# Two layers of a hybrid decoder on one core: TensorE's operands at other places modulo 512 bytes

## The chip, the core and the metric

The kernel runs on one core of a Trainium2 chip. Its time is the device time of one execution in microseconds. Five engines of the core matter here: TensorE (PE in the profile, its weight loads as PEld), VectorE (DVE), ScalarE (ACT), GpSimd (POOL) and SyncE (SP), whose queue issues most of the DMAs. SBUF is the on-chip memory from which TensorE reads both operands of a matmul: the stationary one, which a weight load brings into the array, and the moving one, which streams through it.

## The reference, cut to what matters

The reference is a decoder trunk of two layers on 256 tokens with 1,024 features, all in float32. In each layer

```
xn = rmsnorm(h);  z = xn @ w_in            # 8,200 columns in all
y_b = mixer_b(z_b)                         # RWKV-7, dilated attention, mLSTM, HGRN2
h = h + (sum_b sigmoid(gate_b) * (y_b @ P_b)) @ w_out
h = h + (silu(gt) * u) @ w_down            # u, gt: convolved halves of rmsnorm(h) @ w_up
```

and a last rmsnorm gives the output. Nearly all of the arithmetic is in the products with w_in, the four P_b, w_out, w_up and w_down.

## The kernel before, in words

The activations lie with features on the 128 partitions and tokens along the free axis: a tile of 8 blocks of 256 tokens holds 1,024 features. For the products each operand x is split in two float32r tiles, hi (x rounded) and lo (x - hi), and a product is three matmuls that add up in one PSUM tile: hi x hi, hi x lo, lo x hi. The helper `mm3` issues them (L351 to L353). Weights come in 312 groups of at most 1,024 columns: SyncE's queue loads a group to `raw` (L291), ScalarE makes `hi` from it (L301), VectorE makes `lo` (L302). The groups go round through three raw tiles and four pairs of hi and lo; a queue of four split groups stands ahead of TensorE.

In most products the weights are stationary (128 x 128) and the activations move (256 columns). In the token products (`tok_group`: hgt, att, mlt) and in the last layer's w_down it is the other way round: the activations are stationary, and 512 columns of weights move (392 in att).

These are the sets of activations that TensorE reads in those products, with the names in the profile:

- xh, xl: the inputs before their norm is applied (tags A and B of the persistent pool; made by `norm_block`, L407 and L408). They feed rw, part of hgq and hgf, and the first up groups of each layer.
- sh, sl: the normed inputs (tags C and D; `split_scaled`). They feed the gates, at, ml, the token products and most of up.
- yh, yl: the mixers' outputs, for the projections pp.
- mh, ml_: the merged branches, for w_out (wo).
- ahi, alo: the gated half of the feed-forward part, for w_down (dn).

A stage's matmuls follow one another without other work between them, except where a mixer's small matmuls are put in: the mixers are generators, and a step of one is run after every second call of `step()`. In the stages up, dn and wo nothing is put in apart from the norm's few matmuls (psrf, psbf) and, in the last layer, transposes of h (pht).

SBUF is laid out by pools that stand one behind the other in each partition: constants, weights (raw, hi, lo), the persistent pool (which begins with pr0 and then an empty tile, pad0), small pools, and in each layer a pool of parameters, and behind it the mixers' pools or those of the feed-forward part. A tile's address is the sum of the sizes ahead of it. Five empty tiles stand ahead of tiles that TensorE reads: pad0 (L244, ahead of hT, acc and the sets xh, xl), padC (L442, ahead of sh, sl), pady (L537, ahead of yh, yl), padm (L576, ahead of mh, ml_) and pada (L1410, ahead of ahi, alo). Blocks of the activations are 1,024 bytes long, so all blocks of a set have the same place modulo 512. The blocks of the weights' hi and lo lie at 256 modulo 512, but for att: its second block of 392 columns starts 1,568 bytes behind the first, at 288.

Of the kernel before, what the change touches and what calls it, by code (L numbers as in the profile page):

```python
# [9 lines left out]
F32 = mybir.dt.float32  # L10
# [211 lines left out]
def trunk(tc, x, wst, prm, rows, lora, fing, cfd, cid, out, dbg=None, depth=DEPTH):  # L222
# [7 lines left out]
    pp = pool("persist", bufs=1)  # L230
# [10 lines left out]
    ident_t = cp.tile([128, 128], F32, name="ident_t")  # L241
    pr0 = pp.tile([128, 8], F32, name="pr0")

    pp.tile([128, 416 // 4], F32, name="pad0")  # L244
    hT = pp.tile([128, KB, T], F32, name="hT")
    cft = cp.tile([128, cfd.shape[1] - 128], F32, name="cft")
    cit = cp.tile([128, cid.shape[1]], I32, name="cit")
# [30 lines left out]
    def pad(pl, name, nbytes):  # L278

        pl.tile([128, nbytes // 4], F32, name=name)  # L280
# [32 lines left out]
    def w_next():  # L313
        i = ws["use"]
        ws["use"] += 1
        w_ahead(i + 6)
        while ws["split"] < min(i + 4, NG):
            with tc.high_priority(offset=W_OFF):
                w_split(ws["split"])
            ws["split"] += 1  # L320
        return his.pop(i)
# [6 lines left out]
    def step():  # L328
        beat["t"] += 100
        if beat["t"] < BEAT:  # L330
            return
        beat["t"] -= BEAT
        for e in list(bg):
            e[2] += e[1]
            while e[2] >= 100 and e in bg:
                e[2] -= 100
                try:
                    next(e[0])
                except StopIteration:
                    bg.remove(e)  # L340
# [14 lines left out]
    def ct_block(ps_out, hi, lo, kn, cols, c0, ah, al, k0=0, first=True, last=True, quiet=False):  # L355
        for k in range(kn):
            a = k * cols + c0
            mm3(ps_out, hi[:, a:a + 128], lo[:, a:a + 128], ah[:, k0 + k, :], al[:, k0 + k, :],
                first and k == 0, last and k == kn - 1)
            if not quiet and k % 4 == 3:  # L360
                step()
# [77 lines left out]

    def split_scaled(m, tmp):  # L440
        if m == 0:
            pad(pp, "padC", 448)  # L442
            X["s"] = (pp.tile([128, KB, T], F32R, name="sh", tag="C"), pp.tile([128, KB, T], F32R, name="sl", tag="D"))
        h, lo = X["s"]
        ac.copy(h[:, m, :], tmp)
        gp.tensor_tensor(lo[:, m, :], tmp, h[:, m, :].bitcast(F32), op=OP.subtract)  # L446

    def scaled_block(m, gcol, R, tmp):

        if m % 2:  # L450
            ac.activation(tmp, hT[:, m, :], AF.Copy, scale=gcol)
            gp.tensor_tensor(tmp, tmp, R, op=OP.mult)
        else:
            ve.scalar_tensor_tensor(tmp, hT[:, m, :], gcol, R, op0=OP.mult, op1=OP.mult)
        split_scaled(m, tmp)
# [36 lines left out]
    for l in range(depth):  # L492
        with ExitStack() as lx:
# [12 lines left out]
            with ExitStack() as mxs:  # L506
                mp = lambda name, **k: mxs.enter_context(tc.tile_pool(name=f"{name}{l}", **k))
# [26 lines left out]
                    ve.tensor_scalar(c_ka, P("ka", 0, 2), -1.0, 1.0, op0=OP.mult, op1=OP.add)  # L534
                    ve.tensor_scalar(c_mu, P("mu", 0, 7), -1.0, 1.0, op0=OP.mult, op1=OP.add)

                pad(mp("pady", bufs=1), "pady", 160)  # L537
                yp = mp("yp", bufs=2)
                gtp = mp("gtp", bufs=5)
                zp = mp("zp", bufs=1)  # L540
# [14 lines left out]
                def project(b, kn, m2, quiet=False):  # L555
                    hi, lo = w_next()
                    ps = pmm.tile([128, 2, T], F32, name=f"pp{b}{m2}", tag="mm")
                    for n in range(2):
                        ct_block(ps[:, n, :], hi, lo, kn, 256, n * 128, *res[b], quiet=True)
                    if not quiet:  # L560
                        step()
                    g = gts.pop((b, m2))
                    if b == 3 and m2 == 0:
                        mg["t"] = pp.tile([128, 8, T], F32, name="merged", tag="A")
                    sl = slice(m2 * 2, m2 * 2 + 2)
                    mo = mg["t"][:, sl, :]
                    if b == 3:
                        ve.scalar_tensor_tensor(mo, g, 1.0, ps, op0=OP.add, op1=OP.mult)
                        return
                    ve.scalar_tensor_tensor(g, g, 1.0, ps, op0=OP.add, op1=OP.mult)  # L570
                    if b:
                        gp.tensor_tensor(mo, mo, g, op=OP.add)  # L572
                        return
                    if m2 == 0:
                        mop = mp("mop", bufs=1)
                        pad(mop, "padm", 128)  # L576
                        X["m"] = (mop.tile([128, KB, T], F32R, name="mh"), mop.tile([128, KB, T], F32R, name="ml_"))
                    mh, ml_ = X["m"]
                    ve.tensor_tensor(mo, mo, g, op=OP.add)
                    ac.activation(mh[:, sl, :], mo, AF.Copy, scale=0.5)  # L580
                    ve.scalar_tensor_tensor(ml_[:, sl, :], mo, 0.5, mh[:, sl, :].bitcast(F32), op0=OP.mult, op1=OP.subtract)
# [779 lines left out]
                for m2 in range(4):  # L1361
                    project(3, 2, m2)
                    gates(1, (m2,))
# [14 lines left out]
                for m2 in range(4):  # L1378
                    project(1, 1, m2)
                    gates(2, (m2,))  # L1380
                for e in LAST:
                    if e[0] == "g":
                        gates(0, (e[1],))
                    else:
                        if e == (2, 0):
                            drain(gm)
                            sph.close()
                        if e == (0, 0):
                            drain(grw)
                        project(e[0], 2, e[1])  # L1390
# [16 lines left out]
            with ExitStack() as fxs:  # L1407
                fp = lambda name, **k: fxs.enter_context(tc.tile_pool(name=f"{name}{l}", **k))
                ap_ = fp("act", bufs=1)
                pad(ap_, "pada", 448)  # L1410
                ahi = ap_.tile([128, NJ, T], F32R, name="ahi")
                alo = ap_.tile([128, NJ, T], F32R, name="alo")
                fq = fp("ffq", bufs=2)
# [4 lines left out]
                for j in range(NJ):  # L1418
# [12 lines left out]
                    if j < JU:  # L1431
                        ps = (ps0, ps1)[j] if j < 2 else ct_group(f"up{j}", quiet=True, pool_tag="mx", a=u)
                        z = fq.tile([128, 2, T], F32, name="zf", tag="zf")
                        for cs_, p_ in ps:
                            ve.tensor_tensor(z[:, cs_], p_, bc2(R, cs_.stop - cs_.start), op=OP.mult)
                        if j == 0:
                            for m in range(8):
                                gp.tensor_tensor(xsc[:, m, :], xsc[:, m, :], R, op=OP.mult)  # L1438
                        elif j < 3:
                            for m in range(j * 4 - 4, j * 4):  # L1440
                                split_scaled(m, xsc[:, m, :])
                    else:
                        z = ct_group(f"up{j}", quiet=True, pool_tag="mx")[0][1]
# [117 lines left out]
```

## Time and profile before

| | |
|---|---|
| median of 3 runs | 959.06 us (953.47, 961.19, 959.06) |
| the profiled execution | 950.05 us, of which the span of its instructions 948.3 us |
| mean granted clock of TensorE | 0.994 |
| busy: TensorE / VectorE / ScalarE / GpSimd | 98% / 77% / 60% / 24% |
| HBM | 166 GB/s over the span |

The profile is of one execution. Busy time counts overlapping instructions once; matmuls are pipelined, so TensorE may be busy all the time and still start its matmuls at a faster or slower rate.

### The profile page before, as it was taken

Reading aid. Unit: us, or ns where it says so; the run is one execution under the profiler, and the core shown is the slowest. Engines: PE = TensorE matmul, PEld = TensorE weight load, DVE = VectorE, ACT = ScalarE, POOL = GpSimd, SP = SyncE. Lnnn points to the kernel's source line nnn. Section 1 sums busy time; section 2 is a strip of 40 time slices with the busy share of each in tenths; the row PEclk is TensorE's granted clock in tenths of the full one; section 3 lists DMA queues with packets and bytes.
Section 4 is the critical chain, followed back from the end, with each engine's and each line's share of the span. In section 5 each row is a group of like instructions: output and inputs, shape, how many; then the busy total and the mean of one; then the engine's idle time right before and its main releaser. Section 6 shows DMA issues by size and latency. Waiting matters only on the chain.

```text
span 948.3 us, 21794 instructions
## 1 busy us (share of the span) xinstructions
PE 925.2 (98%) x8880; PEld 874.9 (92%) x8880; DVE 727.2 (77%) x1148; ACT 564.5 (60%) x956; POOL 225.7 (24%) x230
## 2 busy tenths in 40 slices
PE   8899999999999999999999999999999999999996
PEld 6889999999999999999998899999989999999885
DVE  6899556678688998876688975668768889988643
ACT  7773454665466677665479444555745657766532
POOL 3500131111207722120051003101112474111002
PEclk9999999999999999999999999999999999999999
DMA  7544344445466466655655434443546646756651
GB/s 278 178 133 139 113 155 144 135 153 170 135 191 205 144 207 219 199 183 194 207 176 178 134 109 141 147 155 124 169 132 196 200 138 214 232 183 197 188 193 63
DMA packets 48979, 160.08 MB, mean 169 GB/s; under 512 B 5872, under 2 KB 7408, under 8 KB 48752
## 3 DMA queue, kind: packets, MB, share of 16 engines
q1 hardware_dynamic: 46800, 155.03, 50.3%
q10 hardware_dynamic: 1728, 2.62, 0.9%
q8 instruction: 69, 1.13, 0.5%
q0 software_dynamic: 352, 1.06, 0.4%
q14 instruction: 30, 0.25, 0.1%
HBM read 156.06 MB, written 1.05 MB: 166 GB/s over the span
## 4 chain that ended last, share of the span: by engine, by line
PE 75%; DVE 8%; ACT 5%; POOL 4%; DMA 4%; issue 3%; POOLq 0%; ACTq 0%; SPq 0%; DVEq 0%
PE up L353 6%; PE up L351 6%; PE up L352 6%; PE gate L351 6%; PE gate L352 5%; PE gate L353 5%; PE dn L351 4%; PE dn L353 4%; PE dn L352 4%; DVE lo L302 3%; DMA raw<-in_wst_dram 3%; POOL sl L446 2%; ACT hi L301 2%; POOL xsc L1438 2%; PE at L351 1%
## 5 line engine op out<-in xcount | busy, mean ns | idle before, releaser
L302 DVE TENSOR_TENSOR lo<-raw,hi 128x1024 fp32r<-128x1024 f32 (+4 forms) x316 | 375.9, 1195 | 156.0 <-ACT hi L301 147.2
L301 ACT CAST hi<-raw 128x1024 fp32r<-128x1024 f32 (+4 forms) x316 | 307.8, 978 | 268.1 <-PE gate L352 56.9
L353 PE MATMUL up<-sh,lo 128*128 128x256 f32 x544 | 150.8, 277 | 0.7 <-DVE lo L302 0.7
L351 PE MATMUL up<-sh,hi 128*128 128x256 f32 x544 | 150.4, 277 | 0.0
L352 PE MATMUL up<-sl,hi 128*128 128x256 f32 x544 | 150.3, 276 | 0.0
L351 PE MATMUL gate<-sh,hi 128*128 128x256 f32 x512 | 146.0, 285 | 0.0
L352 PE MATMUL gate<-sl,hi 128*128 128x256 f32 x512 | 142.9, 279 | 0.0
L353 PE MATMUL gate<-sh,lo 128*128 128x256 f32 x512 | 142.9, 279 | 0.0
L353 PEld LDWEIGHTS up<-sh,lo 128*128 128x128 f32 x544 | 102.1, 188 | 1.5 <-DVE lo L302 1.5
L352 PEld LDWEIGHTS up<-sl,hi 128*128 128x128 f32 x544 | 102.2, 188 | 0.0
L351 PEld LDWEIGHTS up<-sh,hi 128*128 128x128 f32 x544 | 102.1, 188 | 0.0
L351 PEld LDWEIGHTS gate<-sh,hi 128*128 128x128 f32 x512 | 96.3, 188 | 2.9 <-ACT hi L301 0.2
L352 PEld LDWEIGHTS gate<-sl,hi 128*128 128x128 f32 x512 | 96.2, 188 | 0.9
L353 PEld LDWEIGHTS gate<-sh,lo 128*128 128x128 f32 x512 | 96.2, 188 | 0.6
L1463 POOL TENSOR_TENSOR af<-sf,cvf 128x256 f32<-128x256 f32 x44 | 45.6, 1036 | 154.5 <-ACT sf L1461 154.5
L1459 DVE SCALAR_TENSOR_TENSOR cvf<-up,pr,cvf 128x255 f32<-128x255 f32 (+1 forms) x136 | 65.1, 479 | 2.4
L572 POOL TENSOR_TENSOR merged<-merged,gt 128x512 f32<-128x512 f32 x16 | 25.8, 1614 | 114.0 <-DVE gt L570 109.6
L352 PE MATMUL dn<-alo,hi 128*128 128x256 f32 x176 | 48.5, 276 | 0.0
L353 PE MATMUL dn<-ahi,lo 128*128 128x256 f32 x176 | 48.5, 276 | 0.0
L351 PE MATMUL dn<-ahi,hi 128*128 128x256 f32 x176 | 48.4, 276 | 0.0
L352 PE MATMUL up<-xl,hi 128*128 128x256 f32 x160 | 44.8, 281 | 0.0
L353 PE MATMUL up<-xh,lo 128*128 128x256 f32 x160 | 44.6, 279 | 0.1
(470 smaller groups left out, 2370.7 us busy)
## 6 DMA issues: line engine op xcount, KB each, us to landing
raw<-in_wst_dram SPq DMA_DIRECT2D x254, 512.0 KB, 3.5
raw<-in_wst_dram SPq DMA_DIRECT2D x16, 448.0 KB, 3.2
raw<-in_wst_dram SPq DMA_DIRECT2D x26, 256.0 KB, 2.8
raw<-in_wst_dram SPq DMA_DIRECT2D x8, 392.0 KB, 3.1
zrot<-zrot ACTq DMA_DIRECT2D x24, 64.0 KB, 3.0
cft<-in_cf_dram SPq DMA_DIRECT2D x1, 1041.0 KB, 6.9
hT<-in_x_dram SPq DMA_DIRECT2D x4, 256.0 KB, 5.8
raw<-in_wst_dram SPq DMA_DIRECT2D x8, 128.0 KB, 2.6
```

The costliest lines, as they stand in the source:

```text
L301: ac.copy(hi[:, c], r[:, c])
L302: ve.tensor_tensor(lo[:, c], r[:, c], hi[:, c].bitcast(F32), op=OP.subtract)
L351: te.matmul(o, lh, rh, start=first, stop=False)
L352: te.matmul(o, lh, rl, start=False, stop=False)
L353: te.matmul(o, ll, rh, start=False, stop=last)
L446: gp.tensor_tensor(lo[:, m, :], tmp, h[:, m, :].bitcast(F32), op=OP.subtract)
L572: gp.tensor_tensor(mo, mo, g, op=OP.add)
L1438: gp.tensor_tensor(xsc[:, m, :], xsc[:, m, :], R, op=OP.mult)
L1459: ve.scalar_tensor_tensor(cv[:, n, d:], z[:, n, 0:T - d], P("fcw", 44 * i + cj), cv[:, n, d:], op0=OP.mult, op1=OP.add)
L1463: gp.tensor_tensor(a_, s, cv[:, 0, :], op=OP.mult)
```

## The change

Five empty tiles get another size, one of them a size for each layer. Nothing else is edited.

```diff
-    pp.tile([128, 416 // 4], F32, name="pad0")
+    pp.tile([128, 384 // 4], F32, name="pad0")
...
-            pad(pp, "padC", 448)
+            pad(pp, "padC", 96)
...
-                pad(mp("pady", bufs=1), "pady", 160)
+                pad(mp("pady", bufs=1), "pady", 32)
...
-                        pad(mop, "padm", 128)
+                        pad(mop, "padm", 320)
...
-                pad(ap_, "pada", 448)
+                pad(ap_, "pada", (64, 128)[l])
```

In the built programs the sets then lie at these places modulo 512 bytes:

| set | before | after | after, counted from the weights' 256 |
|---|---|---|---|
| xh, xl (and hT, acc) | 192 | 160 | 416 |
| sh, sl | 192 | 320 | 64 |
| yh, yl | 192 | 192 | 448 |
| mh, ml_ | 192 | 384 | 128 |
| ahi, alo, layer 0 | 192 | 448 | 192 |
| ahi, alo, last layer | 192 | 0 | 256 |
| weights hi, lo (first blocks) | 256 | 256 | 0 |

The tiles behind them in the same pools move along: zf, cvf, sf, af and xsc of the feed-forward part with ahi and alo, the parameters' pr, rowt, lort and hpar to 320 and 384. The mixers' tiles behind pady are shifted by 512 bytes and keep their places. No instruction changes its order on any engine, and none is added or removed.

## Rows read from the trace of the kernel before

**Rows 1.** The page: busy us (share) xinstructions; TensorE and its clock in slices.

```profile
PE 925.2 (98%) x8880; PEld 874.9 (92%) x8880; DVE 727.2 (77%) x1148; ACT 564.5 (60%) x956; POOL 225.7 (24%) x230
PE   8899999999999999999999999999999999999996
PEclk9999999999999999999999999999999999999999
```

**Rows 2.** The page: the chain that ended last, by engine and by line.

```profile
PE 75%; DVE 8%; ACT 5%; POOL 4%; DMA 4%; issue 3%; POOLq 0%; ACTq 0%; SPq 0%; DVEq 0%
PE up L353 6%; PE up L351 6%; PE up L352 6%; PE gate L351 6%; PE gate L352 5%; PE gate L353 5%; PE dn L351 4%; PE dn L353 4%; PE dn L352 4%; DVE lo L302 3%; DMA raw<-in_wst_dram 3%; POOL sl L446 2%; ACT hi L301 2%; POOL xsc L1438 2%; PE at L351 1%
```

**Rows 3.** Groups by form on TensorE: count | busy us, mean ns of one | idle.

```profile
L351 PE MATMUL up<-sh,hi 128*128 128x256 f32 x544 | 150.4, 277 | 0.0
...
L351 PE MATMUL gate<-sh,hi 128*128 128x256 f32 x512 | 146.0, 285 | 0.0
...
L351 PE MATMUL up<-xh,hi 128*128 128x256 f32 x160 | 44.3, 280 | 0.0
...
L351 PE MATMUL dn<-hi,ahi 128*128 128x512 f32 x88 | 32.4, 389 | 0.0
...
L1451 PE MATMUL pht<-ident_t,hT 128*128 128x128 f32 x16 | 2.4, 273 | 0.0
```

**Rows 4.** Timeline of TensorE (start us, us, ...): ends of a long stretch.

```profile
335.79 0.29 PE L352 MATMUL up<-sl,hi 128*128 128x256 f32 x1
335.92 0.28 PE L353 MATMUL up<-sh,lo 128*128 128x256 f32 x1
336.04 0.28 PE L351 MATMUL up<-sh,hi 128*128 128x256 f32 x1
...
482.69 0.28 PE L352 MATMUL rw<-xl,hi 128*128 128x256 f32 x1
```

**Rows 5.** Timeline of TensorE: first row and end of two other stretches.

```profile
304.40 0.28 PE L353 MATMUL up<-xh,lo 128*128 128x256 f32 x1
...
326.55 0.28 PE L352 MATMUL up<-sl,hi 128*128 128x256 f32 x1
...
734.14 0.28 PE L353 MATMUL wo<-mh,lo 128*128 128x256 f32 x1
...
759.47 0.93 PE L1451 MATMUL pht<-ident_t,hT 128*128 128x128 f32 x7
```

**Rows 6.** Windows of these stretches: us, busy us (count) by engine, PEclk, DMA, GB/s.

```profile
304.40:326.55 22.15, 22.15 (x191) 22.15 (x189) 19.67 (x24) 13.19 (x27) 18.82 (x18) 1.00 0.47 146
336.04:482.69 146.65, 146.65 (x1297) 146.65 (x1295) 113.75 (x179) 92.76 (x148) 24.51 (x28) 1.00 0.64 205
734.14:759.47 25.33, 25.33 (x218) 25.33 (x217) 22.48 (x27) 16.83 (x27) 11.44 (x11) 1.00 0.65 203
```

**Rows 7.** Timeline of TensorE: att, starts of two blocks in a row.

```profile
135.23 0.34 PE L351 MATMUL att<-hi,sh 128*128 128x392 f32 x1
...
135.76 0.34 PE L351 MATMUL att<-hi,sh 128*128 128x392 f32 x1
...
136.31 0.34 PE L351 MATMUL att<-hi,sh 128*128 128x392 f32 x1
```

**Rows 8.** Groups by form on ScalarE, columns as in rows 3.

```profile
L407 ACT ACTIVATE xh<-hT,pr 128x256 fp32r<-128x256 f32 x32 | 14.9, 501 | 3.1 <-DMA hT<-in_x_dram 2.1 <-DVE hT L1398 0.9
...
L658 ACT ACTIVATE mixt<-zr,pr 128x256 f32<-128x256 f32 x14 | 7.0, 507 | 4.0 <-DVE zr L659 1.8 <-DVE zr L610 0.9 <-DVE zr L648 0.7
```

**Rows 9.** DMA issues: out<-in, queue, count, KB each, median us to landing.

```profile
raw<-in_wst_dram SPq DMA_DIRECT2D x26, 256.0 KB, 2.8
...
hT<-in_x_dram SPq DMA_DIRECT2D x4, 256.0 KB, 5.8
```

## The prediction

> **What bounds the kernel.** Start with the page's busy line and its slices [rows 1]: TensorE is busy 98% of 948.3 us, at 0.8 or more in every slice but the last, and the granted clock at 0.9 or more in all. Then the chain that ended last [rows 2]: 75% of it is TensorE, the largest other shares being VectorE's 8% and ScalarE's 5%. So the time of this kernel is, most of all, the number of matmuls times the time from one matmul's start to the next one's, which I call the pace. The busy column does not give the pace: the groups [rows 3] show about 277 ns for one matmul of 256 columns, but these overlap. The pace must be read from starts in the timeline.
>
> It has two values. From 336.04 to 482.69 us, 1,294 steps pass without a break [rows 4]: 146.65 us / 1,294 = 113.3 ns. [...] I sorted the steps behind all 5,904 matmuls of three-product form and 256 columns by the timeline's starts: 4,648 are at 112 to 115 ns, 974 at 116 to 121 ns, 282 longer (restarts and waits). A stretch keeps its pace until some other matmul or a wait breaks it. The pace is not fixed by a tile's place alone: the output product wo reads mh and ml_ from one place in both layers, yet runs at 117.8 ns in the second [rows 5], while in the first 178 of 192 steps are at 113 ns.
>
> By the set that is read as the moving operand (short steps of about 113 ns / long ones of about 118 ns): xh and xl 486/407; sh and sl 3,161/341; mh and ml_ 189/186; ahi and alo 528/0; yh and yl, which keep their place, 284/40.
>
> **What the change does, part by part.** No instruction is added, removed or reordered; only addresses differ. So the sum has one kind of term: how many steps change pace, times 117.8 - 113.3 = 4.5 ns.
>
> *Does a place matter at all?* One pair of rows says so. The token product att takes weights of 392 columns, so its second block starts 1,568 bytes behind the first: the moving operand lies at 256 and then at 288 modulo 512, everything else being alike. Three matmuls of the first take 135.76 - 135.23 = 0.53 us, three of the second 136.31 - 135.76 = 0.55 us [rows 7]; in ns of the same starts it is 533 or 534 and 546 or 547, in all undisturbed pairs. That is some 4.5 ns for one matmul, as much as between the two paces, for a shift by 32 bytes.
>
> *xh, xl (192 to 160).* This is the only set that comes to an odd multiple of 32 bytes, like att's second block. I take it that its 486 short steps become long: 486 x 4.5 ns = **+2.2 us**. Ends: none turns (0), or all 407 long ones become short (-1.8 us).
>
> *sh, sl (192 to 320).* 3,696 matmuls, two thirds of all. Its new place is a multiple of 64 like the old one, and no row shows a matmul of this shape there. I take 0. Ends: its 341 long steps become short, -1.5 us; its 3,161 short ones become long, +14.2 us.
>
> *mh, ml_ (384); ahi, alo (448 in layer 0).* Again multiples of 64; 0. Ends together: -0.8 us (186 steps) and +3.2 us (717 steps). In the last layer ahi and alo (now at 0) are the stationary operand beside weights of 512 columns, 264 matmuls of some 390 ns each [rows 3], and sh and sl are that for 192 more; their mean step is 229 ns, and one stretch of hgt shows 233 ns. Taken 0; ends +-4 ns x 456 = +-1.8 us.
>
> *The other engines.* They read and write the same moved tiles. ScalarE's L658 reads blocks 257 elements apart, so at a new place modulo 512 each time, and takes 507 ns, against 501 ns for L407 on even blocks of the same size [rows 8]. So I cost their moves at nothing; the cover is TensorE's 98%.
>
> *DMA.* hT now starts at 160. Its four transfers land 5.8 us after issue, and the first matmul waits for them; a weight transfer of the same 256 KB lands after 2.8 us [rows 9], later and alone. I take no change; half a microsecond either way would be hidden in the ends above.
>
> Sum: the profiled execution took 950.05 us (948.3 us of span and 1.75 around it); + 2.2 = 952.3 us. The median of the three runs, 959.06 us, stands 9.0 us above the profiled one, so the forecast beside that median is **961 us**, no change that can be told: a measurement of this kernel tells about 1%, 9.6 us, from none (the three runs lie 7.7 us apart).
>
> [...]
>
> **Rivals.**
>
> *No place counts.* The two paces then come from the phase in which a stretch happens to restart, as wo's two layers suggest. 959 us, give or take the 4.2 us that all long steps of the moved sets are worth (934 x 4.5 ns).
>
> *The new places bring the 117.8 ns pace to stay (slower).* Mechanism: matmul and weight load run side by side, the load lagging by some ns, and read from two places of the same partitions; their distance modulo 512 was the same, 192 against 256, for all the matmuls that I counted. The change makes it a different one for each moved set. If each of them meets what now meets only the stretches at 117.8 ns, 3,161 + 189 + 528 + 486 = 4,364 steps x 4.5 ns = +19.6 us: 979 us, 2.0% slower. It decides from 9.6 / 0.0045 = 2,130 steps on, so only if sh and sl are among them; they alone give +14.2 us, 973 us. For it: the long undisturbed stretches at 113.3 ns [rows 4] were all read at 192, and att. Against it: those stretches are broken by restarts and come back at 113.3 ns by themselves in most cases.
>
> *A third, longer pace.* After restarts, single steps of 121 to 124 ns occur, as the two before 336.04 us [rows 4]. If such a step became a lasting state for sh and sl, 3,161 x 9 ns = +28 us: 987 us.
>
> *A better pace (faster).* Transposes of 128 columns, each with a weight load too [rows 1], come at (0.93 - 0.273) / 6 = 109 ns, the 0.273 us being one transpose's own busy time [rows 3, 5]. If some place gave that to all moved sets, 5,568 x 4.3 ns = 24 us, and the long steps' 4.2 us, come off: 931 us. Against it: no step of the 5,904 was under 112 ns, and a transpose moves half the bytes. A gain of over 1% needs it: without it, the best is 955 us.
>
> [...]
>
> **How the numbers follow.** Chances: forecast (xh and xl at 117.8 ns, the rest as it is) 0.26, 961 us; no place counts 0.30, 959 us; every long step gone 0.10, 955 us; 117.8 ns for sh and sl or for all 0.24, 973 to 979 us; a third, longer pace 0.05; a better pace 0.05. The first three differ by less than can be measured and form one case, whose middle is 960 us; I keep 961. The first three make 0.66 for no change; scatter between runs takes 0.01 of that to the faster side and 0.01 to the slower: faster 0.06, same 0.64, slower 0.30. The range goes from 952 (all long steps gone, and 3 us of scatter) to 981 us (all moved sets at 117.8 ns, and 2 us of scatter); beyond lie the last two cases and a little scatter.
>
> **What the next profile would show.** Right: steps of 113.3 ns in the long stretches on sh and on ahi, 117.8 ns on xh, unchanged means of L301 and L302 and of the gaps of TensorE. The rival on the slower side: 117.8 ns, or some third value, through the whole of the stretch that follows the restart near 336 us. A better pace: anything under 112 ns there. I am wrong, too, if another engine's mean changes, or if TensorE idles at a place where it does not now; then a place matters to more than TensorE's reads.

## The result, and the profile after

The changed kernel takes 966.39 us (median of 8 runs, 964.11 to 970.03) beside 957.81 us for the kernel before: ratio 1.0112, 95% interval 1.0083 to 1.0141 (the two medians by themselves lie 8.6 us, 0.9%, apart). That is 1.1% slower, at the edge of what a measurement can tell from none, inside the range of 952 to 981 us, and above the forecast of 961. What came is the rival on the slower side, with two exceptions that are told below.

The page of the changed kernel, the lines that answer to [rows 1, 2]:

```profile
PE 942.4 (98%) x8880; PEld 892.7 (93%) x8880; DVE 728.5 (76%) x1148; ACT 564.5 (59%) x956; POOL 226.2 (23%) x230
...
PEclk9999999999999999999999999999999999999998
...
PE 91%; DVE 3%; DMA 2%; ACT 2%; issue 1%; POOL 1%; POOLq 0%; SPq 0%; ACTq 0%; DVEq 0%
```

TensorE's busy time grew by 17.2 us for the same 8,880 matmuls, the other engines' by 1.3 us at most, and the chain is now 91% TensorE instead of 75%. Nothing else became slower; TensorE got further ahead as the bound. Its groups by form (count | busy us, mean ns of one | idle), to be read against [rows 3]:

```profile
L351 PE MATMUL up<-sh,hi 128*128 128x256 f32 x544 | 152.3, 280 | 0.0
L351 PE MATMUL gate<-sh,hi 128*128 128x256 f32 x512 | 147.9, 289 | 0.0
L351 PE MATMUL dn<-ahi,hi 128*128 128x256 f32 x176 | 48.5, 276 | 0.0
L351 PE MATMUL up<-xh,hi 128*128 128x256 f32 x160 | 44.6, 282 | 0.0
L351 PE MATMUL wo<-mh,hi 128*128 128x256 f32 x128 | 35.7, 284 | 0.3 <-ACT gt L550 0.3
L351 PE MATMUL dn<-hi,ahi 128*128 128x512 f32 x88 | 32.5, 390 | 0.0
```

Two of them are not in [rows 3]; before they were:

```profile
L351 PE MATMUL dn<-ahi,hi 128*128 128x256 f32 x176 | 48.4, 276 | 0.0
L351 PE MATMUL wo<-mh,hi 128*128 128x256 f32 x128 | 35.0, 280 | 0.0
```

The groups shown with 256 moving columns rose by 2 to 4 ns, but for dn with ahi, at 276 ns as before; the one of dn with 512 moving columns rose by 1 ns. The pace stands in the timeline's starts, as in [rows 4]. A step is the time from a matmul's start to the next one's, a restart the first matmul behind a break. First the stretch on sh that follows the restart near 331 us, then the border between up and dn, then its end:

```profile
331.13 0.28 PE L351 MATMUL up<-sh,hi 128*128 128x256 f32 x1
...
424.05 0.28 PE L351 MATMUL dn<-ahi,hi 128*128 128x256 f32 x1
424.17 0.28 PE L352 MATMUL dn<-alo,hi 128*128 128x256 f32 x1
...
483.90 0.28 PE L351 MATMUL rw<-xh,hi 128*128 128x256 f32 x1
```

From 331.13 to 424.17 us there are 790 steps: 93.04 us / 790 = 117.8 ns, where [rows 4] had 113.3. Before, 117.8 ns stood in the shorter stretches of [rows 5] (215 steps in 25.33 us, 188 in 22.15 us), at the granted clock of 1.00 that the stretch at 113.3 ns had as well [rows 6]. At the border, without a break, the pace becomes (483.90 - 424.17) us / 527 = 113.3 ns. One stretch of matmuls of one shape, at one granted clock (1.00 from 345 to 415 and from 425 to 475 us), runs at two paces, and what differs in the program is where ahi and sh lie. The steps of the 5,904 matmuls, sorted as in the prediction (short: under 115.5 ns; long: from there to under 121; longer: the rest), and the mean of those under 130 ns:

| set | place before, after | short / long / longer before | after | mean ns before, after |
|---|---|---|---|---|
| sh, sl | 192, 320 | 3,161 / 341 / 194 | 124 / 3,395 / 177 | 113.9, 117.6 |
| xh, xl | 192, 160 | 486 / 407 / 67 | 86 / 677 / 197 | 115.5, 118.3 |
| mh, ml_ | 192, 384 | 189 / 186 / 9 | 27 / 224 / 133 | 115.6, 119.3 |
| ahi, alo, layer 0 | 192, 448 | 528 / 0 / 0 | 527 / 1 / 0 | 113.3, 113.3 |
| yh, yl | 192, 192 | 284 / 40 / 12 | 118 / 196 / 22 | 113.9, 116.3 |

Between the two profiles the time goes like this: steps under 130 ns +18.0 us, longer steps, where TensorE waits or restarts, -3.3 us, token products and the last layer's dn under 0.1 us together; sum +14.8 us, and the spans differ by 963.0 - 948.3 = 14.7 us. The runs differ by 1.1% only, some 10.7 us. The profile of before that the prediction had is the least of all its runs, as a second one shows (the experiment before_again): against that the span grew by 963.0 - 952.6 = 10.4 us.

### The profile page after: what moved, and what is told of

It is laid out like the page before. It is cut to its first block, busy times and chain, and to the rows that moved or that the text cites. A ratio compares the mean times of both kernels' runs of the same rounds, so it can differ in the third digit from the quotient of the medians.

```text
span 963.0 us, 21794 instructions
## 1 busy us (share of the span) xinstructions
PE 942.4 (98%) x8880; PEld 892.7 (93%) x8880; DVE 728.5 (76%) x1148; ACT 564.5 (59%) x956; POOL 226.2 (23%) x230
## 4 chain that ended last, share of the span: by engine, by line
PE 91%; DVE 3%; DMA 2%; ACT 2%; issue 1%; POOL 1%; POOLq 0%; SPq 0%; ACTq 0%; DVEq 0%
PE up L353 8%; PE up L351 8%; PE up L352 8%; PE gate L351 7%; PE gate L352 6%; PE gate L353 6%; PE dn L351 4%; PE dn L353 4%; PE dn L352 4%; DMA raw<-in_wst_dram 2%; PE pp L351 1%; PE at L351 1%; PE pp L352 1%; PE pp L353 1%; PE at L352 1%; PE at L353 1%
## 5 line engine op out<-in xcount | busy, mean ns | idle before, releaser
L302 DVE TENSOR_TENSOR lo<-raw,hi 128x1024 fp32r<-128x1024 f32 (+4 forms) x316 | 376.4, 1197 | 166.9 <-ACT hi L301 156.3
L301 ACT CAST hi<-raw 128x1024 fp32r<-128x1024 f32 (+4 forms) x316 | 307.3, 977 | 283.5 <-PE gate L352 53.9
L353 PE MATMUL up<-sh,lo 128*128 128x256 f32 x544 | 152.5, 280 | 0.1
L351 PE MATMUL up<-sh,hi 128*128 128x256 f32 x544 | 152.3, 280 | 0.0
L352 PE MATMUL up<-sl,hi 128*128 128x256 f32 x544 | 152.3, 280 | 0.0
L351 PE MATMUL gate<-sh,hi 128*128 128x256 f32 x512 | 147.9, 289 | 0.0
L352 PE MATMUL gate<-sl,hi 128*128 128x256 f32 x512 | 144.9, 283 | 0.0
L353 PE MATMUL gate<-sh,lo 128*128 128x256 f32 x512 | 144.7, 283 | 0.0
L353 PEld LDWEIGHTS up<-sh,lo 128*128 128x128 f32 x544 | 102.1, 188 | 0.6 <-DVE lo L302 0.4
L351 PEld LDWEIGHTS up<-sh,hi 128*128 128x128 f32 x544 | 102.3, 188 | 0.0
L352 PEld LDWEIGHTS up<-sl,hi 128*128 128x128 f32 x544 | 102.1, 188 | 0.0
L351 PEld LDWEIGHTS gate<-sh,hi 128*128 128x128 f32 x512 | 96.9, 189 | 2.7 <-ACT hi L301 0.2
L352 PEld LDWEIGHTS gate<-sl,hi 128*128 128x128 f32 x512 | 96.9, 189 | 0.9
L353 PEld LDWEIGHTS gate<-sh,lo 128*128 128x128 f32 x512 | 96.7, 189 | 0.7
L353 PE MATMUL dn<-ahi,lo 128*128 128x256 f32 x176 | 48.6, 276 | 0.0
L352 PE MATMUL dn<-alo,hi 128*128 128x256 f32 x176 | 48.6, 276 | 0.0
L351 PE MATMUL dn<-ahi,hi 128*128 128x256 f32 x176 | 48.5, 276 | 0.0
L352 PE MATMUL up<-xl,hi 128*128 128x256 f32 x160 | 45.0, 282 | 0.0
L353 PE MATMUL up<-xh,lo 128*128 128x256 f32 x160 | 44.8, 281 | 0.0
```

The costliest lines, as they stand in the source:

```text
L301: ac.copy(hi[:, c], r[:, c])
L302: ve.tensor_tensor(lo[:, c], r[:, c], hi[:, c].bitcast(F32), op=OP.subtract)
L351: te.matmul(o, lh, rh, start=first, stop=False)
L352: te.matmul(o, lh, rl, start=False, stop=False)
L353: te.matmul(o, ll, rh, start=False, stop=last)
```

## The experiments

The theory, D: the pace depends on the distance modulo 512 between the activations that a matmul streams and the weights that are loaded beside it (in the window below each weight load of the kernel before starts 3 or 4 ns behind a matmul). Rivals: P, the activations' own place counts; N, restarts fall into either pace by chance; and O, for which operand of the weights counts. before_again and hi_448 have one execution each and all_288 two, the others four to ten; the ratios are to executions of the kernel before on the same chip. Each is shown by the same window, 345 to 415 us, which holds nothing but up groups on sh in layer 0; the figure in brackets behind PE is the number of matmuls that touch it, two or three more than start in it. For the kernel before:

```profile
345.00:415.00 70.00, 70.00 (x620) 70.00 (x619) 60.18 (x94) 48.83 (x81) 13.93 (x14) 1.00 0.64 204
```

70 us / 617 = 113.5 ns; the other columns are weight loads, VectorE, ScalarE, GpSimd, granted clock (1.00), DMA share and GB/s.

**sh and sl alone put back** (undo_s):

```diff
-            pad(pp, "padC", 96)
+            pad(pp, "padC", 480)
...
-                pad(mp("pady", bufs=1), "pady", 32)
+                pad(mp("pady", bufs=1), "pady", 160)
...
-                pad(ap_, "pada", (64, 128)[l])
+                pad(ap_, "pada", (192, 256)[l])
```

> The changed kernel with sh and sl alone put back at 192; the other sets stay at their new places. Theory D (what counts is the distance modulo 512 between what a matmul streams and what the weight load beside it reads): the long stretches on sh are back at 113.3 ns a step, those on xh and mh stay at 118 to 120 ns, ahi at 113.3 ns; the time is about 1.003 of before (2.2 us for xh, 1 us for mh, of 958). Rival N (the pace is the chance of a restart, places count for nothing): sh stays at 117.8 ns in a good part of its stretches, ratio 1.005 to 1.011.

```profile
345.00:415.00 70.00, 70.00 (x620) 70.00 (x619) 61.06 (x96) 49.20 (x81) 12.66 (x13) 1.00 0.64 205
```

Ratio to before 1.0016 (0.9986 to 1.0046), 3,127 of 3,696 steps on sh short again. xh and mh keep their long steps (711 and 225). As D has it: the loss is in sh and sl.

**sh and sl alone moved** (only_s):

```diff
-            pad(pp, "padC", 448)
+            pad(pp, "padC", 64)
...
-                pad(mp("pady", bufs=1), "pady", 160)
+                pad(mp("pady", bufs=1), "pady", 32)
...
-                pad(ap_, "pada", 448)
+                pad(ap_, "pada", 320)
```

> The kernel before with sh and sl alone moved to 320; xh, mh, ahi and yh stay at 192. Theory D: sh runs at 117.8 ns everywhere (some 3,150 steps more than in the profile of before, 14 us against that profile), ratio 1.008 to 1.015, nearly all of the changed kernel's 1.011. Rival: if the loss came from the small sets (xh, mh) or from other tiles that moved, the ratio is 1.003 or less and sh runs at 113.3 ns. Rival N: ratio 1.000 to 1.01, sh in a mix of both paces.

Windows 345 to 415 us (up on sh) and 425 to 475 us (dn on ahi):

```profile
345.00:415.00 70.00, 70.00 (x597) 70.00 (x596) 59.00 (x93) 47.74 (x79) 12.81 (x13) 1.00 0.65 200
425.00:475.00 50.00, 50.00 (x427) 50.00 (x426) 31.03 (x38) 25.70 (x39) 6.77 (x7) 1.00 0.58 187
```

Ratio 1.0143 (1.0096 to 1.0189): the whole loss, from one set. It is not less than the changed kernel's, for a reason that D alone did not foresee: ahi, left at 192, runs at 50 us / 424 = 117.9 ns as well; all its 528 steps are long. dn starts behind up without a break and inherits the pace, and at 192 that pace lasts. In the changed kernel ahi at 448 shed it at the border. So a place does not fix a pace; a stretch can keep the state that it is in. Why it was kept at 192 and shed at 448 stays open: the two places are alike in all_448 below, which has unbroken stretches of 188 and 179 long steps at 448.

**The weights moved instead** (weights_128):

```diff
-    pp.tile([128, 416 // 4], F32, name="pad0")
+    pp.tile([128, 32 // 4], F32, name="pad0")
...
+    cp.tile([128, 384 // 4], F32, name="padw")
     acc = pp.tile([128, 2, T], F32, name="acc")
```

> The kernel before with the weights' tiles raw, hi and lo moved from 256 to 128 modulo 512 by an empty tile, all sets of activations still at 192: the distance is 64 for every set, as for sh and sl in the changed kernel, but the activations' own places are those of before. Theory D: 117.8 ns on sh, ratio 1.010 to 1.020. Rival P (the place of the activations by itself counts, 320 is bad and 192 good): 113.3 ns in the long stretches, ratio 1.000 within 0.003. Rival N: ratio 1.000, a mix.

```profile
345.00:415.00 70.00, 70.00 (x597) 70.00 (x596) 59.44 (x93) 48.48 (x80) 12.78 (x13) 1.00 0.64 202
```

Ratio 1.0154 (1.0107 to 1.0201), with all sets at the very places of before. P is out: the place of the activations alone does not decide, and this one move of the weights gives what D asks for. But 612 steps on sh are short here, 479 of them in one stretch at the end of up in the last layer; so 113.3 ns can last at distance 64 too, and most restarts do not end there.

**All sets at 448** (all_448), pad0 of before cut from 416 to 160 bytes:

> The kernel before with pad0 alone cut by 256 bytes, so that every set lies at 448 (distance 192, as ahi in layer 0 of the changed kernel); the mixers' own tiles move by 256 too. Theory D: 113.3 ns on all sets, xh and mh included; if no restart ends in 117.8 ns the ratio is 0.993 to 0.997 and the runs scatter less than those of before. Rival N: the same mix as before, ratio 1.000 within 0.003, the long stretches on xh or mh in part at 117.8 ns.

```profile
345.00:415.00 70.00, 70.00 (x620) 70.00 (x619) 60.85 (x96) 49.52 (x82) 12.74 (x13) 1.00 0.65 204
```

Ratio 0.9996 (0.9968 to 1.0025): no gain. The counts are 4,639 short and 972 long, before 4,648 and 974, though other stretches are long. Distances 192 and -64 behave alike.

**All sets at 256, at 0, at 64** (pad0 480, 224, 288 bytes):

> The kernel before with pad0 64 bytes larger: every set at 256, distance 0, where moving operand and weight load begin at the same place modulo 512. So far 113.3 ns and 117.8 ns have both been lasting states at distances -64, 64 and 192, and the distance decided in which of them most restarts end. Theory D: distance 0 has a mix of its own, between ratio 0.993 (113.3 ns after every restart) and 1.018 (117.8 ns throughout); if the loads and the streams collide most when they start at one place, it is near the upper end. Rival N: the mix of before, 1.000 within 0.003.

```profile
345.00:415.00 70.00, 70.00 (x585) 70.00 (x585) 58.01 (x92) 46.98 (x77) 12.65 (x13) 1.00 0.64 197
```

> The kernel before with pad0 192 bytes smaller: every set at 0, distance 256. If the pattern repeats every 256 bytes (192 and -64, which differ by 256, gave nearly the same step counts: 4,639 and 4,648 short ones), this equals distance 0 step for step and its ratio equals that of the run at 256 within 0.003. If the period is 512, the two differ.

```profile
345.00:415.00 70.00, 70.00 (x586) 70.00 (x585) 57.97 (x91) 46.81 (x78) 12.53 (x13) 1.00 0.61 199
```

> The kernel before with pad0 128 bytes smaller: every set at 64, distance -192. With a period of 256 bytes this is distance 64 again, the one of sh and sl in the changed kernel and of the weights at 128: mostly 117.8 ns, ratio 1.010 to 1.018. With a period of 512 it may be anything; with rival P (the activations' own place counts) it says nothing of 64 or 320.

```profile
345.00:415.00 70.00, 70.00 (x596) 70.00 (x596) 59.12 (x93) 47.28 (x79) 12.72 (x13) 1.00 0.62 199
```

Ratios 1.0232 (1.0213 to 1.0250), 1.0215 (1.0197 to 1.0232) and 1.0139 (1.0121 to 1.0158). Distances 0 and 256 give one state, 120.0 ns: 70 us / 583 = 120.1, and in the timeline of the first the starts follow at 120 ns each:

```profile
400.02 0.28 PE L351 MATMUL up<-sh,hi 128*128 128x256 f32 x1
400.14 0.28 PE L352 MATMUL up<-sl,hi 128*128 128x256 f32 x1
400.26 0.28 PE L353 MATMUL up<-sh,lo 128*128 128x256 f32 x1
400.38 0.28 PE L351 MATMUL up<-sh,hi 128*128 128x256 f32 x1
```

In the window from 345 to 415 us all 583 steps of the run at 256 are 120 ns, among them 68 in which VectorE does nothing, 166 in which ScalarE does nothing and 34 in which no DMA packet is under way. So what the other engines read and write at the time, a rival without a run of its own, does not make these steps long.

31 and 29 steps of 5,904 are short. Distance -192 is 64 over again on sh (574 short steps, most of them in the same last stretch, beside 612); on xh the two are less alike (5 short steps beside 184). So in these three pairs (0 and 256, 64 and -192, -64 and 192) the pattern repeats every 256 bytes. The prediction took all multiples of 64 for alike; what told was the distance modulo 256.

**The kernel before again** (before_again), unedited:

> The kernel before, unedited, for a second profile of it. If the pace is set anew at each restart by chance, other stretches than in the first profile run at 117.8 ns (then wo in the last layer, or the first up groups on xh, may be short this time), and the count of long steps differs by several hundred from 974, which is what the scatter of its runs (950 to 961 us) would ask for: 9 us are 2,000 steps. If restarts always end the same way, the counts agree within some tens.

```profile
345.00:415.00 70.00, 70.00 (x620) 70.00 (x620) 60.62 (x96) 49.08 (x81) 12.57 (x13) 1.00 0.64 204
```

1,152 long steps beside 974: wo in the last layer is short this time, and several of sh's stretches are long that were short, the longest of 187 steps near 801 us. N holds for single restarts. But the span, 952.6 us, is 4.3 us longer than the first, and the steps are not what made it so: those under 130 ns are 0.6 us less in sum, the longer ones 3.4 us more, the token products 1.1 us more. The expectation that the scatter of the runs asks for 2,000 steps is wrong; between these two profiles waits and restarts make most of the difference. The largest difference is one wait, which the first profile has at 0.5 us:

```profile
PE psw L699 <- DVE la L671: 2.1, 1, 2.1
```

**All sets at 224, 288 and 352** (pad0 448, 512, 64 bytes), the odd multiples of 32:

> The kernel before with pad0 32 bytes larger: every set at 224, distance -32 (224 of 256). Measured so far, by distance modulo 256: 0 gives 120.0 ns throughout, 64 mostly 117.8, 192 mostly 113.3. Theory D with a period of 256 sees 224 between 192 and 0: if the pace rises from 192 to 0 in steps, most steps are between 113.3 and 120 ns, ratio 1.000 to 1.023. If the odd multiple of 32 is what costs (as in att's second block), it is above 192 in any case. A version that beats the kernel before would show under 974 long steps and a ratio under 0.996; I give that one chance in five.

```profile
345.00:415.00 70.00, 70.00 (x593) 70.00 (x593) 59.00 (x93) 46.87 (x78) 12.76 (x13) 1.00 0.58 197
```

> The kernel before with pad0 96 bytes larger: every set at 288, distance 32. Theory D: between 0 (120.0 ns) and 64 (117.8 ns), so 118 to 120 ns and a ratio of 1.015 to 1.023. If odd multiples of 32 have a price of their own, above 1.023.

```profile
345.00:415.00 70.00, 70.00 (x602) 70.00 (x602) 59.62 (x95) 48.21 (x80) 12.73 (x13) 1.00 0.62 202
```

> The kernel before with pad0 352 bytes smaller: every set at 352, distance 96, the one multiple of 32 below 128 not yet measured. Steps so far by distance modulo 256: 0 120.0 ns, 32 116.9, 64 mostly 117.8, 192 mostly 113.3, 224 118.3; from sets of the changed kernel 128 119.3 and 160 118.2. Theory D: 192 alone is good, so 116 to 120 ns here and a ratio of 1.010 to 1.023. If 113.3 ns were the usual pace and only some distances bad, the ratio is 1.000 or less; I give that one chance in ten.

```profile
345.00:415.00 70.00, 70.00 (x586) 70.00 (x585) 58.63 (x92) 47.40 (x78) 13.04 (x13) 1.00 0.63 201
```

Ratios 1.0177 (1.0121 to 1.0234), 1.0134 (1.0062 to 1.0205) and 1.0257 (1.0193 to 1.0320). Here the single steps alternate (115 to 125 ns at 352) about means of 118.3, 116.9 and 119.9 ns. No odd multiple is good, but 288, at 1.0134, is better than 256 at 1.0232 and no worse than 64 at 1.0139: being odd showed no price of its own. The hope for a better version fell three times over.

**hi alone at the bad distance** (hi_448):

```diff
-    pp.tile([128, 416 // 4], F32, name="pad0")
+    pp.tile([128, 224 // 4], F32, name="pad0")
...
+    wp.tile([128, 192 // 4], F32, name="padh", tag="padh", bufs=1)
     ve.memset(warm, 0.0)
```

> The kernel before with the hi tiles of the weights alone moved to 448 (distance 192 - 448 = -256, that is 0 modulo 256, the 120.0 ns place), lo still at 256 (distance -64), all activations at 192. Of the three matmuls of a product the first two (L351, L352 of before) have hi as their stationary operand, the third (L353) lo; the weight load that runs beside a matmul is the next one's: hi beside L351 and L353, lo beside L352. Theory D says that the load beside counts: steps of L351 and L353 are long (near 120 ns), those of L352 short. Rival O (the matmul's own stationary place counts): L351 and L352 long, L353 short. If the state is one of the whole sequence, all three are alike, near (120 + 120 + 113.3) / 3 = 117.8 ns.

```profile
345.00:415.00 70.00, 70.00 (x596) 70.00 (x596) 58.98 (x93) 47.56 (x79) 12.77 (x13) 1.00 0.60 199
```

The one execution took 967.97 us. Only 45 steps are short, and in up on sh the three matmuls of a product are nearly alike: 117.5, 117.6 and 118.3 ns for L351, L352 and L353 of before. Neither D's split (L352 short) nor O's (L353 short) shows; the third case does, one state of the whole sequence near 117.8 ns. Two thirds of the loads at a bad distance lengthen all three steps; whether the load beside a matmul or its own stationary operand counts is still open, and so is what inside the chip makes the step longer.

The means of sh's steps under 130 ns, all sets at one distance modulo 256 (128 and 160 are single sets of the changed kernel, mh and xh):

| distance | 0 | 32 | 64 | 96 | 128 | 160 | 192 | 224 |
|---|---|---|---|---|---|---|---|---|
| ns | 119.8 | 116.9 | 117.1 | 119.9 | 119.3 | 118.3 | 113.9 | 118.3 |

192, the one that the kernel before has, is the only good one of the eight, and restarts at it still end in the longer pace at times; no version that was run beats it.

## Why the prediction was right or wrong, point by point

- *TensorE's pace is the bound.* Right: +18.0 us in steps under 130 ns against 14.7 us of span, the other engines unchanged: ScalarE's L301 takes 977 ns after 978, VectorE's L302 1,197 after 1,195.
- *xh, xl: 486 short steps become long, +2.2 us.* Right in sign and nearly in size: 400 did, the mean rose by 2.8 ns, some 2.5 us. The reason, an odd multiple of 32, was wrong: 160 is bad among bad ones, and 288, odd as well, is less bad than 256. The att rows, from which it was taken, turn round in the changed kernel, where sh lies at 320 and the weights' blocks still at 256 and 288. The pair below takes 541 ns at 256 and 526 ns at 288 (before 533 and 547), and the other undisturbed pairs there have this order by 11 to 21 ns or differ by 2 to 4 ns; in all_256 it is 533 and 534. So att, too, went by how the two operands lie to each other, and it has their roles exchanged.

```profile
129.69 0.34 PE L351 MATMUL att<-hi,sh 128*128 128x392 f32 x1
...
130.23 0.34 PE L351 MATMUL att<-hi,sh 128*128 128x392 f32 x1
...
130.76 0.34 PE L351 MATMUL att<-hi,sh 128*128 128x392 f32 x1
```

- *sh, sl: I take 0.* This is the step that failed. It took the upper end: 3,037 short steps went, the mean rose by 3.7 ns, 13 us. "No row shows a matmul of this shape there" was true, and 0 was then the choice of a middle without a reason; the bound of +14.2 us was good, as only_s shows (1.0143).
- *mh, ml_ and ahi, alo: 0.* One of each: mh rose to a mean of 119.3 ns, 1.4 us, more than the 117.8 ns that bounded it, and ahi stayed at 113.3 ns. *yh, yl keep their place*, so they had no term; they lost 166 short steps (0.8 us), and since their few matmuls stand among gates on sh, they seem to take over the pace of these, as ahi did in only_s.
- *Token products and the last dn: +-1.8 us.* They cancel: +0.6 us with sh at 320, -0.5 us with ahi at 0.
- *The other rivals.* "No place counts" is refuted by all_256, where pad0 alone changed: 120.0 against 113.3 ns for the same instructions. The 120 ns steps of all_256 are the same with VectorE, ScalarE or DMA at rest (68, 166 and 34 steps). What is left, by elimination, is how TensorE's own two operands lie to each other; that their reads hinder each other is a guess, which no run shows. "A better pace" did not come at any of eight distances: no kernel has a lasting step of this shape under 113.3 ns, and the 109 ns of the transposes was not reached.
- *The point from which it decides.* Right that it takes sh and sl. But 2,130 steps would not have been enough: the changed kernel has 3,766 short steps fewer than the profile of before (4,648 to 882), worth 18.0 us, and is 1.1% slower, since steps and time do not go one to one (next point).
- *The sum against the median.* The 9.0 us between the profiled run and the median were added as if the change worked on the median's execution. The waits that make an ordinary run longer than that profile shrink when TensorE is slower: longer steps gave back 3.3 us against the first profile of before and 6.6 us against the second. That is why, against before_again, 18.6 us of steps cost 10.4 us of span (1.1 us more came off in the token products and the last dn). That the time came out 5 us from the forecast, inside the range, is in good part luck: a term of 13 us on sh was missing, and shorter waits and a base that was too high (959.06 us for a kernel whose eight runs have a median of 957.81) hid much of it.

## What to carry to other kernels

When TensorE is the bound and each matmul of 256 float32r columns has its own weight load, look at the time from start to start: two paces at one shape and one clock can point to where the operands lie, though chance at a restart gives two as well. Keep the distance between moving operand and weights constant modulo 256 bytes, measure a few distances with one empty tile (here 113.9 to 119.9 ns, ratios up to 1.026), and check after each edit of the pools that it did not move. Read a pace from long undisturbed stretches, and mind that a stretch can inherit it from the one ahead, as dn in only_s did (117.9 ns, at the place where it had 113.3).

## What the runs showed of the hardware that was not expected

- In the pairs measured the pattern repeats every 256 bytes: 120.0 ns at distances 0 and 256, short and long counts of 4,648 / 974 and 4,639 / 972 at -64 and 192.
- The paces are lasting states with memory: at one distance both 113.3 and 117.8 ns can last for hundreds of steps (weights_128: 479 at 113.3 and 1,294 at 117.8), and dn at an unchanged place ran at 117.8 ns behind an up that did. What makes a stretch shed an inherited pace, as dn at 448 did, is not shown.
- Exchanging the operands' roles changes the good places: with 512 columns of weights moving, ahi at 0 instead of 192 shortened the mean step from 229 to 227 ns, while sh at 320 lengthened that of mlt from 229 to 234 ns. For that dn the distance modulo 256, counted from the stationary activations to the moving weights, again orders the runs: 226.8 ns at 0 (all_256, all_0 and the changed kernel), 228.9 at 64 (before and all_448), 233.3 at 192 (weights_128 and all_64). So a distance that is among the worst for 256 moving columns (0, at 119.8 ns beside 119.9 at 96) is the best of these three here.
